# Transposes through two-bank PSUM tiles, norm gains stored by row, and moved norms and weights in a two-layer decoder trunk

## The chip, the cores and the metric

The kernel runs on one core of one Trainium2 chip. The metric is the device time of one execution in microseconds (us). Three runs of the kernel before took 2549.63 us in the median (2548.11 to 2550.36). About 0.2% is what a measurement of it can tell from no change.

## The reference

Two layers over 1024 tokens of width 1024, all in float32:

```python
for layer in range(2):
    hn = rms_norm(h, norm_mix[layer])
    h = h + (diff_attention if layer == 0 else gla)(hn, ...)      # 8 heads / 4 heads
    h = h + conv_ffn(rms_norm(h, norm_ffn[layer]), w_up, conv_w, conv_b, w_down)
return rms_norm(h, norm_final)

def rms_norm(x, gain):   # in float32
    return x * lax.rsqrt(jnp.mean(x * x, axis=-1, keepdims=True) + 1e-6) * gain

def diff_attention(...):     # per head: q, k, v = h @ w_qkv; rope on q and k; two causal softmaxes
    a = p[0] - lam * p[1]
    o = rms_norm(a @ v, subln_gain) * (1 - lambda_init)           # then all heads @ w_o

def conv_ffn(h, ...):        # d_ff = 2816
    u = causal_depthwise_conv(h @ w_up, width=3) + conv_b
    gate, up = jnp.split(u, 2, axis=-1)
    return (silu(gate) * up) @ w_down
```

## The kernel before, in words

**Numbers.** Every factor of a large product is split into a high and a low part, and a product is three matmuls into one float32 PSUM tile (`mm3`, L142 to L144: high by high, low by high, high by low). ACT writes the high part by a copy, DVE or POOL the low part by a subtraction. This is so for weights (`split_w`, L122 and L123; `UpWeights.block`, L477 and L478), for the normed activations (`XH` and `XL`) and for what the heads give (`gh` and `gl`).

**PSUM.** There are two pools, eight banks in all: `psm`, four tiles of one bank of 128x512 (`mm_ps`), and `psb`, two tiles of two banks of 128x1024 (`big_ps`). A tile is given out again when all readers of its last use are done.

**Order.** A scheduler orders the instructions of each engine when the kernel is built. `in_order` (L135) binds pieces of TensorE's work behind one another by hand. Weights of the projections are loaded two ahead (`prefetch`, L106). All loads and stores go through SP's queue.

**The start.** Eight blocks `xt` of x (128 tokens each) are loaded, with the gain of the first norm between the first and the second (`load_gain`, L165, which reads one row of 4 KB into all 128 partitions). Per block ACT squares (L170), DVE and POOL make `rs` (L172, L174), DVE scales to `hn` (L179), TensorE transposes (L202), ACT and DVE write XH and XL. Then come the q and k products of the first head, `stack_q` and `stack_k` (which set the two maps of a head one below the other by DMA; the low parts `ql` and `kl` are POOL's), and v.

**Attention, last head.** `finish` (L796) squares one half of a head's output; its closure `rest` (norm by rows, `rstd_rows`, and the write through `proj.put`) is kept in `later`. Beside the last head's blocks runs the output projection's first part over k = 0 and 1 (`first_units`). After the heads, `OutProjection.rest` (L395) adds k = 2, 3, 4 for tiles 2 and 6 (`accumulate_tiles`, four banks), runs what is left of the last head's norm, and goes on with tiles 3, 7, 0, 4, 1, 5 one by one.

**The block transposes.** In the second half of `rest`, k = 5, 6, 7 are added for tiles t and t + 4 in turn. ACT squares the tile into a two-bank tile (`squares`), and the normed rows `h0` and `h1` are cut into halves. The FFN's up-projection uses a seven-product scheme on blocks, so the operands are not only A11, A12 (`first_row`) and A22 but also the sums S1 to S4 (`Blocks.sums`). Each is transposed by `Blocks.put` (L230): four 128x128 transposes into one bank, one ACT copy, one or two DVE subtractions. That is 28 transposes for each t of 0 to 3. The last five operands of t = 3 (`last_blocks`) come between the first products of the FFN's unit f = 0.

**The FFN.** For each of 22 units f: products `ps_x`, `ps_y`, `ps_z`, and meanwhile the seven weight blocks of f + 1 (`UpWeights.sums`, `others`; DVE L486 to L493). Then the down-projection adds groups of units, (0, 1) first, tile by tile, `accumulate_tile` into two of the four single banks.

Of the kernel before, what the change touches and what calls it, by code (L numbers as in the profile page):

```python
# [46 lines left out]
def trunk(ctx, tc, x, norm_mix, norm_ffn, norm_final, wqk, wv, w_o, lam_in, subln,  # L47
# [117 lines left out]
    def load_gain(src):  # L165
        return staged(src.broadcast_to([P, D]))
# [45 lines left out]
    class Blocks:  # L212
# [17 lines left out]
        def put(self, n, src, t):  # L230
            pt = mm_ps("pt")
# [4 lines left out]
            for (k, hi), (_, lo) in zip(*self.parts(n)):  # L236
                ks = pv[:, k:k + hi.shape[1], :]
                nc.scalar.copy(hi[:, :, tok], ks)
                nc.vector.tensor_tensor(lo[:, :, tok], ks, f32(hi[:, :, tok]), op=ALU.subtract)  # L239
# [17 lines left out]
        def others(self, blocks, t):  # L257
            for n, src in blocks:
                self.put(n, src, t)
# [29 lines left out]
    def accumulate_tiles(res, ts, pairs):  # L289

        ps = [mm_ps("pacc") for _ in range(2 * len(ts))]
# [41 lines left out]
    class OutProjection:  # L333
# [35 lines left out]
        def first_units(self):  # L369
# [14 lines left out]
            def unit(t):  # L384
# [5 lines left out]
                if t == late[0]:  # L390
                    self.prepare((2,))
            return [begin] + [lambda t=t: unit(t) for t in (*early, *late)]

        def rest(self, gain_src, up):

            layer, res = self.layer, self.res
            self.prepare((3, 4))
            pairs = [self.pairs[k] for k in (2, 3, 4)]
            for n, t in enumerate((2, 6, 3, 7, 0, 4, 1, 5)):
                if n != 1:  # L400
                    with in_order(n == 0):
                        (accumulate_tiles(res, (2, 6), pairs) if n == 0 else accumulate_tile(res, t, pairs))
                if n == 1:
                    while self.late:
                        with in_order():
                            self.late.pop(0)()
                if t % 4 > 1:
                    nc.sync.dma_start(r_scr[layer, t], res[t])
# [93 lines left out]
    def ffn(layer, X, last_blocks, up, gain_src, after):  # L502
# [65 lines left out]
        for f in range(NF):  # L568
# [5 lines left out]
            if f + 1 < NF:  # L574
                up.sums(f + 1)
# [56 lines left out]
    def rope_stack_units(h, st, parts=False):  # L632
# [31 lines left out]
        def stack_k():  # L664
            kl = slot(12, "kl", F32R)
            nc.scalar.copy(KS[0], roped[1])
            nc.gpsimd.tensor_tensor(kl, roped[1], f32(KS[0]), op=ALU.subtract)
# [47 lines left out]
    def attention(st, proj, value_T):  # L715
# [49 lines left out]
        def transposes(h, i, a):  # L765
# [3 lines left out]
            for j0 in range(0, i + 1, 4):  # L769
                n = min(4, i + 1 - j0)  # L770
                pt = mm_ps("pta")
# [24 lines left out]
        def finish(h, hf):  # L796
            o = oT[h]
            a = slot(13, "sq", F32, [P, 2, 512])
            nc.scalar.activation(a[:, 0, :], o, AF.Square)
            on = slot(27, "on")[:, :512]  # L800
            nc.scalar.mul(on, o, st["sub"])
            hl = split_rows(a[:, 0, :], 26)
# [9 lines left out]
            later.append(rest)  # L812
# [10 lines left out]
        for h in range(HEADS):  # L823
# [17 lines left out]
            if h + 1 == HEADS:  # L841
                drain()
                proj.late = later
# [470 lines left out]
```

## Time and profile before

| what | us |
|---|---|
| median of three runs | 2549.63 |
| the profiled execution | 2550.43 |
| its span, first to last instruction | 2548.7 |
| TensorE busy (PE) | 2459.1 (96%) |
| VectorE busy (DVE) | 1617.3 (63%) |
| GpSimd busy (POOL) | 1183.6 (46%) |
| ScalarE busy (ACT) | 1041.2 (41%) |
| mean granted TensorE clock | 0.985 |

The span and the median are read against one another thus: the profiled execution lies 0.80 us above the median, and 1.73 us of it lie outside the span. A row of the view by stretches gives, for each engine, its busy time and its instructions in brackets, then the mean granted TensorE clock, the busy share of the DMA engines and what they moved. A row of the timeline gives the start, the time, the engine, the line, the operation, the tile written and those read, the sizes, the count, and in brackets the engine's idle time ahead of it and what ended that.

### The profile page before, as it was taken

The page shows a single profiled execution, that of the slowest core. Times are in us where ns is not written, and L with a number is a line of the kernel's source. Part 1 is how long each engine was busy: PE and PEld are TensorE (multiplying, and loading weights), DVE is VectorE, ACT ScalarE, POOL GpSimd, SP SyncE. Part 2 cuts the span into 40 slices and gives each one's busy share as a digit, 9 for nine tenths or more (in the row PEclk, how much of TensorE's full clock was granted, in tenths as well). Part 3 has the DMA queues.
Part 4 walks back from the last instruction along what each step waited for, and adds up shares of the span by engine and source line. Part 5 has one row for each costly group of instructions (what it writes and reads, how often), then busy time and mean ns, then how long its engine had stood idle before and what let it go on. Part 6 is the DMA issues. An engine that isn't in the chain of part 4 may idle for free. (4 is left out here: it accounts for less than half of the span.)

```text
span 2548.7 us, 30815 instructions
## 1 busy us (share of the span) xinstructions
PE 2459.1 (96%) x11752; PEld 2001.0 (79%) x11752; DVE 1617.3 (63%) x2218; ACT 1041.2 (41%) x1638; POOL 1183.6 (46%) x723
## 2 busy tenths in 40 slices
PE   7999999988899999999999999998889999999998
PEld 5777777767688888878888998987768888887887
DVE  5577777875666666655565576487566666665445
ACT  4454445543454445421124443442345544443211
POOL 3444444424555555545423344343455555555441
PEclk9999999999899999999999999999989999999999
DMA  5222222433122222343321111124212222234331
GB/s 178 63 67 59 59 58 59 126 126 108 66 86 80 83 77 90 126 156 116 100 86 59 34 42 58 34 91 157 100 66 87 79 83 77 89 129 154 114 100 66
DMA packets 66020, 228.61 MB, mean 90 GB/s; under 512 B 8144, under 2 KB 8784, under 8 KB 65872
## 3 DMA queue, kind: packets, MB, share of 16 engines
q1 hardware_dynamic: 65872, 226.64, 27.0%
q8 instruction: 92, 1.51, 0.3%
q14 instruction: 56, 0.46, 0.1%
HBM read 163.17 MB, written 50.86 MB: 84 GB/s over the span
## 5 line engine op out<-in xcount | busy, mean ns | idle before, releaser
L308 DVE TENSOR_TENSOR res<-pacc,res 128x512 f32<-128x512 f32 x408 | 279.4, 689 | 271.5 <-PE pacc L144 271.0
L478 POOL TENSOR_TENSOR uw<-st,uw 128x512 fp32r<-128x512 f32 x190 | 288.4, 1518 | 240.6 <-ACT uw L477 227.7
L123 POOL TENSOR_TENSOR wl<-st,wh 128x1024 fp32r<-128x1024 f32 x55 | 140.2, 2554 | 211.7 <-ACT wh L122 207.8
L142 PE MATMUL pacc<-wdh,gh 128*128 128x512 f32 x512 | 200.2, 393 | 4.0 <-DVE res L308 4.0
L143 PE MATMUL pacc<-wdl,gh 128*128 128x512 f32 x512 | 201.7, 394 | 0.1
L144 PE MATMUL pacc<-wdh,gl 128*128 128x512 f32 x512 | 201.6, 394 | 0.0
L557 DVE SCALAR_TENSOR_TENSOR b<-cu,cv,b 128x1023 f32<-128x1023 f32 x44 | 62.4, 1419 | 186.7 <-ACT b L556 186.7
L477 ACT CAST uw<-st 128x512 fp32r<-128x512 f32 x190 | 118.1, 622 | 112.8 <-PE ps_z L144 55.6
L142 PE MATMUL psq<-XH,wh 128*128 128x512 f32 x384 | 156.1, 407 | 1.2 <-DVE ms L172 1.2
L604 POOL TENSOR_TENSOR gl<-st,gh 128x1024 fp32r<-128x1024 f32 x32 | 78.8, 2463 | 164.5 <-ACT gh L603 121.9
L143 PE MATMUL psq<-XL,wh 128*128 128x512 f32 x384 | 153.9, 401 | 0.8 <-DVE ms L172 0.7
L144 PE MATMUL psq<-XH,wl 128*128 128x512 f32 x384 | 152.6, 399 | 0.0
L753 ACT ACTIVATE p<-p,nmax 128x256 f32<-128x256 f32 (+7 forms) x128 | 99.0, 776 | 86.7 <-DVE nmax L750 85.5
L142 PE MATMUL pacc<-wh,gh 128*128 128x512 f32 x256 | 106.0, 417 | 18.5 <-DVE XL L239 10.9
L603 ACT CAST gh<-st 128x1024 fp32r<-128x1024 f32 x32 | 33.6, 1050 | 214.8 <-PE pacc L143 141.9
L478 POOL TENSOR_TENSOR wh<-st,wh 128x512 fp32r<-128x512 f32 x56 | 86.1, 1537 | 69.6 <-ACT wh L477 69.6
L142 PEld LDWEIGHTS pacc<-wdh,gh 128*128 128x128 f32 x512 | 96.5, 188 | 26.1 <-DVE res L308 5.3
L478 POOL TENSOR_TENSOR wl<-st,wl 128x512 fp32r<-128x512 f32 x56 | 84.1, 1502 | 66.8 <-ACT wl L477 64.7
L143 PEld LDWEIGHTS pacc<-wdl,gh 128*128 128x128 f32 x512 | 96.6, 189 | 22.9 <-POOL wdl L604 1.0
L144 PEld LDWEIGHTS pacc<-wdh,gl 128*128 128x128 f32 x512 | 96.4, 188 | 21.0
L122 ACT CAST wh<-st 128x1024 fp32r<-128x1024 f32 x59 | 61.6, 1047 | 121.7 <-PE psq L143 51.4
L750 DVE CUSTOM_DVE_ANT_0 p<-s_ps,mask 128x256 f32<-128x256 f32 (+7 forms) x128 | 91.4, 750 | 26.9 <-PE pta L773 22.6
(357 smaller groups left out, 7384.8 us busy)
## 6 DMA issues: line engine op xcount, KB each, us to landing
st<-in_wup_dram SPq DMA_DIRECT2D x88, 512.0 KB, 3.5
g_scr<-a SPq DMA_DIRECT2D x44, 512.0 KB, 2.6
st<-in_wdn_dram SPq DMA_DIRECT2D x44, 512.0 KB, 3.6
st<-g_scr SPq DMA_DIRECT2D x44, 512.0 KB, 3.3
r_scr<-res SPq DMA_DIRECT2D x24, 512.0 KB, 3.2
res<-r_scr SPq DMA_DIRECT2D x24, 512.0 KB, 5.6
st<-in_wqk_dram SPq DMA_DIRECT2D x16, 512.0 KB, 3.6
st<-o_scr SPq DMA_DIRECT2D x13, 512.0 KB, 3.3
```

What stands on the lines that cost most here:

```text
L122: nc.scalar.copy(hi, st)
L123: (eng_lo or nc.gpsimd).tensor_tensor(lo, st, f32(hi), op=ALU.subtract)
L142: nc.tensor.matmul(ps, lhsT=ah, rhs=bh, start=first, stop=False, **kw)
L143: nc.tensor.matmul(ps, lhsT=ah, rhs=bl, start=False, stop=False, **kw)
L144: nc.tensor.matmul(ps, lhsT=al, rhs=bh, start=False, stop=last, **kw)
L308: nc.vector.tensor_tensor(res[t][:, half(dh)], ps, res[t][:, half(dh)], op=ALU.add)
L477: nc.scalar.copy(w[:, half(0)], src)
L478: nc.gpsimd.tensor_tensor(w[:, half(1)], src, f32(w[:, half(0)]), op=ALU.subtract)
L557: nc.vector.scalar_tensor_tensor(u[:, 1:], c[:, :T - 1], cv[:, n, 1:2], u[:, 1:], op0=ALU.mult, op1=ALU.add)
L604: nc.gpsimd.tensor_tensor(lo, st, f32(hi), op=ALU.subtract)
L750: nc.vector.tensor_tensor_reduce(out=pm[:, :w], in0=s_ps[:, :w], in1=st["mask"][:, T - w:], scale=-0.125, scalar=3.0e38, op0=ALU.add, op1= ...
L753: nc.scalar.activation(pm[:, :w], pm[:, :w], AF.Exp, bias=nmax, scale=-1.0, accum_out=sums[:, m:m + 1])
```

## The change

1. The gains of the norms lie in memory as 128 equal rows, and `load_gain` reads 512 KB instead of one row of 4 KB.
2. `prefetch()` at the start leaves the low parts of the first two weights to POOL instead of DVE.
3. `stack_q` and `stack_k` of the first head use DVE instead of POOL for `ql` and `kl`.
4. The closures of the last head's `finish` go to `proj.late`, with places in memory of their own for the second half; the last block's transposes use a two-bank tile.
5. `accumulate_tiles` uses all eight banks, for four tiles (2, 6, 3, 7) instead of two, and so do the first groups of the down-projection. In layer 1, k = 3 is prepared in `first_units`.
6. `first_row` transposes eight times into one two-bank tile, with one copy and one subtraction of 128x1024. S3 and S1 (for t = 3 all operands) use the halves of a two-bank tile.
7. The weight sums of f = 1 are bound behind the last blocks' copy and subtraction.

```diff
     def load_gain(src):
-        return staged(src.broadcast_to([P, D]))
+        return staged(src)
...
         def first_row(self, h0, t):
-            for i, n in enumerate(("A11", "A12")):
-                self.put(n, h0[:, half(i)], t)
+            pt = big_ps("pt")
+            for k in range(KT):
+                nc.tensor.transpose(pt[:, k * P:(k + 1) * P], h0[:, k * P:(k + 1) * P], ident)
+            pv = pt.rearrange("p (a b) -> p a b", a=KT)
+            hi, lo = (z[:, :, t * P:(t + 1) * P] for z in (XH, XL))
+            nc.scalar.copy(hi, pv)
+            nc.vector.tensor_tensor(lo, pv, f32(hi), op=ALU.subtract)
...
         def others(self, blocks, t):
-            for n, src in blocks:
-                self.put(n, src, t)
+            big = None
+            for i, (n, src) in enumerate(blocks):
+                if t == 3 or n in ("S3", "S1"):
+                    if big is None:
+                        big = big_ps("pt2")
+                        pt, big = big[:, half(0)], big[:, half(1)]
+                    else:
+                        pt, big = big, None
+                else:
+                    pt = mm_ps("pt")
+                self.put(n, src, t, pt)
...
     def accumulate_tiles(res, ts, pairs):
-        ps = [mm_ps("pacc") for _ in range(2 * len(ts))]
+        ps = [mm_ps("pacc") for _ in range(4)]
+        for _ in range(2):
+            big = big_ps("pacc2")
+            ps += [big[:, half(0)], big[:, half(1)]]
...
+                if t == late[1] and self.base:
+                    self.prepare((3,))
...
-            self.prepare((3, 4))
+            self.prepare((4,) if self.base else (3, 4))
...
-            for n, t in enumerate((2, 6, 3, 7, 0, 4, 1, 5)):
...
+            with in_order(True):
+                accumulate_tiles(res, (2, 6, 3, 7), pairs)
+            for t in (2, 6, 3, 7):
+                nc.sync.dma_start(r_scr[layer, t], res[t])
+            while self.late:
+                with in_order():
+                    self.late.pop(0)()
+            for t in (0, 4, 1, 5):
+                with in_order():
+                    accumulate_tile(res, t, pairs)
...
             if f + 1 < NF:
-                up.sums(f + 1)
+                with ExitStack() as behind:
+                    for i in () if f else X.last:
+                        behind.enter_context(tc.issue_after(i.ins))
+                    up.sums(f + 1)
...
+            if fs[0] == 0:
+                for t in (0, 4):
+                    accumulate_tiles(res, range(t, t + 4), [pairs[f] for f in fs])
+                continue
...
-            nc.gpsimd.tensor_tensor(QL, roped[0], f32(QH[0]), op=ALU.subtract)
+            (nc.vector if parts else nc.gpsimd).tensor_tensor(QL, roped[0], f32(QH[0]), op=ALU.subtract)
...
-            later.append(rest)
+            (proj.late if h == HEADS - 1 else later).append(rest)
...
-            prefetch(nc.vector)
+            prefetch()
```

The rest of the diff: `kl` as `ql`, `finish` with slots 17, 18, 19 for the last half, `pt` handed to `put`, which keeps its last copy and subtraction in `X.last`, and `_rows`, which writes a gain out 128 times on the host's side of the layout.

What moves, at three places. First POOL, at the end of the first head's q, k and v products (`sh`, `qr`, `kr` are the rotation's steps, `wl` the low part of the v weights). Before:

```order
L651 TENSOR_TENSOR sh<-sh,sin 128x512
L659 TENSOR_TENSOR ql<-qr,qh_146 128x1024
L652 TENSOR_TENSOR kr<-kr,sh 128x512
L667 TENSOR_TENSOR kl<-kr,ks_148 128x1024
L123 TENSOR_TENSOR wl<-st,wh 128x1024
```

and now DVE there, where POOL goes from `kr` straight to `wl`:

```order
L676 TENSOR_TENSOR kr<-psq,cos 128x512
L123 TENSOR_TENSOR wl<-st,wh 128x1024
L685 TENSOR_TENSOR ql<-qr,qh_146 128x1024
L693 TENSOR_TENSOR kl<-kr,ks_148 128x1024
L776 ISA p_533,nmax<-s_ps,mask 128x128
```

`ql` no longer stands between two steps of the rotation, and `kl` has left POOL's queue.

Second PE, in the block transposes of the first t (`hn` are the normed rows and their sums in place, `tmp` is S3, `pacc` the accumulation of the next tile; after the first row of transposes, stretches of `pacc` matmuls are left out). Before:

```order
L233 MATMUL pt<-ident,hn 128x128 x8
...
L144 MATMUL pacc<-wh,gl 128x512
L233 MATMUL pt<-ident,hn 128x128 x8
L233 MATMUL pt<-ident,tmp 128x128 x4
L233 MATMUL pt<-ident,hn 128x128 x8
L142 MATMUL pacc<-wh,gh 128x512
```

and now, with 18, 9 and 9 matmuls of `pacc` in the three gaps:

```order
L244 MATMUL pt<-ident,hn 128x128 x8
...
L232 MATMUL pt<-ident,hn 128x128 x12
...
L232 MATMUL pt_5411<-ident,tmp 128x128 x4
...
L232 MATMUL pt_5411<-ident,hn 128x128 x4
L244 MATMUL pt<-ident,hn 128x128 x8
```

The 20 transposes in one run have become 12, 4 and 4 with matmuls between them, and the last 4 stand right ahead of the next tile's first eight.

Third DVE, between the first two products of unit f = 0 and the last blocks (L252 and L253, now L256 and L257, are sums of blocks; L486 to L493, now L505 to L512, the weight sums of f = 1; `cg` drains `ps_y`). Before:

```order
L253 TENSOR_TENSOR hn<-hn 128x512
L486 TENSOR_TENSOR st<-st 128x512
L487 TENSOR_TENSOR st<-st 128x512
L488 TENSOR_TENSOR st<-st 128x512
L493 TENSOR_TENSOR st<-st 128x512
L527 TENSOR_TENSOR cg<-ps_y,rv 128x512
L239 TENSOR_TENSOR XL<-pt,XH 128x4x128
```

and now:

```order
L257 TENSOR_TENSOR hn<-hn 128x512
L546 TENSOR_TENSOR cg<-ps_y,rv 128x512
L238 TENSOR_TENSOR XL<-pt_5763,XH 128x4x128
L238 TENSOR_TENSOR XL<-pt_5663,XH 128x4x128
...
L505 TENSOR_TENSOR st<-st 128x512
L506 TENSOR_TENSOR st<-st 128x512
L507 TENSOR_TENSOR st<-st 128x512
```

The four weight sums have gone behind the last blocks' subtractions.

## Rows read from the trace of the kernel before

**Rows 1.** The page, part 1: busy time of TensorE.

```profile
PE 2459.1 (96%) x11752; PEld 2001.0 (79%) x11752; DVE 1617.3 (63%) x2218; ACT 1041.2 (41%) x1638; POOL 1183.6 (46%) x723
```

**Rows 2.** Busy time by stretches, core 0; after the engines clock, DMA share, GB/s.

```profile
0.00:21.20 21.20, 7.47 (x32) 5.85 (x32) 11.25 (x20) 13.42 (x23) 3.46 (x8) 1.00 0.89 343
54.50:100.00 45.50, 41.98 (x175) 31.17 (x173) 18.56 (x49) 15.49 (x34) 24.14 (x17) 0.89 0.32 82
526.00:560.00 34.00, 27.27 (x133) 21.88 (x133) 27.05 (x35) 15.46 (x22) 12.07 (x6) 0.90 0.37 124
597.00:668.00 71.00, 54.51 (x253) 43.93 (x252) 50.56 (x75) 30.91 (x68) 42.31 (x35) 0.86 0.32 108
1092.00:1106.00 14.00, 11.05 (x42) 8.68 (x41) 14.00 (x11) 5.58 (x6) 8.62 (x4) 0.88 0.45 141
1755.00:1775.00 20.00, 13.83 (x50) 10.25 (x49) 15.17 (x17) 6.20 (x8) 6.67 (x3) 0.83 0.57 190
1811.00:1880.00 69.00, 53.74 (x244) 42.83 (x244) 49.72 (x75) 30.86 (x67) 42.08 (x35) 0.85 0.30 100
2290.00:2335.00 45.00, 43.87 (x189) 34.90 (x188) 28.28 (x32) 18.28 (x19) 34.45 (x13) 1.00 0.69 240
...
2340.00:2500.00 160.00, 160.00 (x694) 130.03 (x693) 77.42 (x112) 28.07 (x28) 66.63 (x28) 1.00 0.27 86
```

**Rows 3.** The page, part 5: DVE's drains of `pacc` (busy, mean ns; idle before).

```profile
L308 DVE TENSOR_TENSOR res<-pacc,res 128x512 f32<-128x512 f32 x408 | 279.4, 689 | 271.5 <-PE pacc L144 271.0
```

**Rows 4.** Timeline of the start, all engines.

```profile
1.63 0.42 SPq L101 DMA_DIRECT2D st<-in_norm_mix_dram  x1
...
8.52 1.28 DVE L179 SCALAR_TENSOR_TENSOR hn<-xt,rs,st 128x1024 f32<-128x1024 f32 x1 [2.69 <-DMA st<-in_norm_mix_dram]
...
17.54 1.22 DVE L123 TENSOR_TENSOR wl<-st,wh 128x1024 fp32r<-128x1024 f32 x1
...
21.24 0.47 PE L142 MATMUL psq<-XH,wh 128*128 128x512 f32 x1 [1.17 <-DVE ms L172]
```

**Rows 5.** Timeline of the first head: POOL, then DVE, then PE.

```profile
50.25 2.16 POOL L652 TENSOR_TENSOR qr<-qr,sh 128x512 f32<-128x512 f32 x1
...
54.53 3.39 POOL L659 TENSOR_TENSOR ql<-qr,qh 128x1024 fp32r<-128x1024 f32 x1
57.89 1.28 POOL L652 TENSOR_TENSOR kr<-kr,sh 128x512 f32<-128x512 f32 x1
60.33 2.40 POOL L667 TENSOR_TENSOR kl<-kr,ks 128x1024 fp32r<-128x1024 f32 x1 [1.16 <-ACT ks L666]
...
49.28 1.97 DVE L123 TENSOR_TENSOR wl<-st,wh 128x1024 fp32r<-128x1024 f32 x1
...
63.92 0.66 PE L681 MATMUL psw<-ident,vt 128*128 128x128 f32 x4 [0.95 <-ACT vt L675]
67.15 0.68 PE L740 MATMUL s_ps<-ks,qh 128*128 128x128 f32 x2 [2.57 <-DMA ks<-kl]
```

**Rows 6.** Timeline at the end of the last head: DVE, then PE.

```profile
533.44 2.29 DVE L286 SCALAR_TENSOR_TENSOR sq<-sq 128x512 f32<-128x512 f32 x1
...
542.86 1.97 PE L773 MATMUL pta<-ident,p 128*128 128x128 f32 x8 [3.94 <-DVE res L308]
```

**Rows 7.** Timeline of the block transposes, layer 0: PE, then DVE.

```profile
609.18 0.47 PE L142 MATMUL pacc<-wh,gh 128*128 128x512 f32 x1 [2.76 <-DVE XL L239]
...
642.78 1.09 PE L233 MATMUL pt<-ident,hn 128*128 128x128 f32 x8 [2.88 <-DVE XL L239]
...
659.02 1.09 PE L233 MATMUL pt<-ident,tmp 128*128 128x128 f32 x4 [4.55 <-DVE cg L527]
...
650.97 1.78 DVE L486 TENSOR_TENSOR st<-st 128x512 f32<-128x512 f32 x1
```

**Rows 8.** Timeline of PE: first down group of layer 0, projection of layer 1.

```profile
1100.56 0.50 PE L142 MATMUL pacc<-wdh,gh 128*128 128x512 f32 x1 [2.95 <-DVE res L308]
...
1765.96 0.80 PE L142 MATMUL pacc<-wh,gh 128*128 128x512 f32 x1 [5.17 <-ACT gh L128]
```

More of the change, by code (lines that the diff above doesn't have):

```diff
@@ L228, in operand, with put @@
             return v[:, k - first, :]
-        def put(self, n, src, t):
-            pt = mm_ps("pt")
+        def put(self, n, src, t, pt):
             for k in range(4):
@@ L237, in put @@
                 ks = pv[:, k:k + hi.shape[1], :]
-                nc.scalar.copy(hi[:, :, tok], ks)
-                nc.vector.tensor_tensor(lo[:, :, tok], ks, f32(hi[:, :, tok]), op=ALU.subtract)
+                self.last = (nc.scalar.copy(hi[:, :, tok], ks),
+                             nc.vector.tensor_tensor(lo[:, :, tok], ks, f32(hi[:, :, tok]), op=ALU.subtract))
         def first_row(self, h0, t):
-            for i, n in enumerate(("A11", "A12")):
-                self.put(n, h0[:, half(i)], t)
+            pt = big_ps("pt")
[5 more added lines that the diff above has]
+            nc.vector.tensor_tensor(lo, pv, f32(hi), op=ALU.subtract)
         def sums(self, h0, h1, t):
@@ L396, in rest @@
             layer, res = self.layer, self.res
-            self.prepare((3, 4))
+            self.prepare((4,) if self.base else (3, 4))
             pairs = [self.pairs[k] for k in (2, 3, 4)]
-            for n, t in enumerate((2, 6, 3, 7, 0, 4, 1, 5)):
[L400 to L408, printed above, removed]
+            with in_order(True):
[8 more added lines that the diff above has]
+                    accumulate_tile(res, t, pairs)
             self.prepare((5, 6, 7))
@@ L666, in stack_k @@
             nc.scalar.copy(KS[0], roped[1])
-            nc.gpsimd.tensor_tensor(kl, roped[1], f32(KS[0]), op=ALU.subtract)
+            (nc.vector if parts else nc.gpsimd).tensor_tensor(kl, roped[1], f32(KS[0]), op=ALU.subtract)
             dma(KS[1][up], KS[0][up])
@@ L770, in transposes @@
                 n = min(4, i + 1 - j0)
-                pt = mm_ps("pta")
+                if h == HEADS - 1 and i == NT - 1:
+                    pt = big_ps("pta")[:, half(0)]
+                else:
+                    pt = mm_ps("pta")
                 for j in range(j0, j0 + n):
@@ L797, in finish @@
             o = oT[h]
-            a = slot(13, "sq", F32, [P, 2, 512])
+            ia, ion, ihl = (17, 18, 19) if h == HEADS - 1 and hf else (13, 27, 26)
+            a = slot(ia, "sq", F32, [P, 2, 512])
             nc.scalar.activation(a[:, 0, :], o, AF.Square)
-            on = slot(27, "on")[:, :512]
+            on = slot(ion, "on")[:, :512]
             nc.scalar.mul(on, o, st["sub"])
-            hl = split_rows(a[:, 0, :], 26)
+            hl = split_rows(a[:, 0, :], ihl)
             def rest():
@@ L842, in attention @@
                 drain()
-                proj.late = later
             value_T = next_v
@@ L1183, in trunk @@
             nc.sync.dma_start(ident, ident_in)
-            gain = load_gain(norm_mix[0:1, :])
+            gain = load_gain(norm_mix[0])
         if t == 3:
-            prefetch(nc.vector)
+            prefetch()
     attention_consts(st)
@@ L1206, in trunk @@
     up = UpWeights(0)
-    X, last_blocks = proj.rest(norm_ffn[0:1, :], up)
+    X, last_blocks = proj.rest(norm_ffn[0], up)
     def keep(t, hn, res):
@@ L1215, in trunk @@
     up = UpWeights(1)
-    X, last_blocks = proj2.rest(norm_ffn[1:2, :], up)
+    X, last_blocks = proj2.rest(norm_ffn[1], up)
     def store(t, hn, res):
@@ L1254, in _units, with _rows @@
     return s
+def _rows(w):
+    return np.ascontiguousarray(np.broadcast_to(w[:, None, :], (w.shape[0], P, D)))
 def _moving(w):
```

8 lines of the change are left out of this document (4 added, 4 removed).

## The prediction, made before the changed kernel was run

> **What bounds the kernel now.** I read the page's busy shares first: TensorE is busy for 2459.1 of 2548.7 us [rows 1], so the program is TensorE's work plus 89.6 us in which it stands still, plus what it loses at half clock. Then the view by stretches. From 2340 to 2500 us 694 matmuls fill 160.00 us without a gap, 0.231 us each [rows 2]; no edit of other engines can gain anything there, and most of the program is like that. What can be gained lies in few stretches, and for each the reader takes two numbers from its row: length less PE busy, which is idle, and (1 - clock) times length, which is work lost to the lower of the two clock levels (1.2 instead of 2.4 GHz: a stretch at half clock shows 0.50). From the rows [rows 2]:
>
> - 0 to 21.2 us: 13.7 idle. 54.5 to 100: 3.5 idle, 5.0 clock.
> - 526 to 560: 6.7 idle, 3.4 clock.
> - 597 to 668 (block transposes, layer 0): 16.5 idle, 9.9 clock.
> - 1092 to 1106: 3.0 idle, 1.7 clock.
> - 1755 to 1775: 6.2 idle, 3.4 clock.
> - 1811 to 1880 (block transposes, layer 1): 15.3 idle, 10.3 clock.
> - 2290 to 2335: 1.1 idle, no clock.
>
> That is 66 us idle and 34 us of clock, 100 us in all: the most that a change of these places could give. The half clock comes behind stalls (of 2.57, 2.76, 3.94 and 5.17 us, [rows 5 to 8]). The third view is the timeline around each stall, which says what ended it: most often DVE, whose drain of one PSUM bank takes 0.69 us [rows 3] and which has other work in its queue.
>
> **The change, part by part.** Gains are negative, and ends of each are given for the range.
>
> *Start (edits 1 and 2).* The first `hn` waits 2.69 us for the gain and starts at 8.52 [rows 4], though the load was issued at 1.63: 6.9 us. TensorE's first transposes need it. As plain rows the gain is one more 512 KB load behind x's first block, so I expect it to be there when `rs` is. It is also ahead of the next three blocks of x. DVE then loses two `wl`, one of them the 1.22 us at 17.54, which stand ahead of the first psq at 21.24 [rows 4]; POOL gets two of some 2.4 us (the length of `kl`, which has that size, [rows 5]) in a queue that otherwise holds `rs`. Sum: 2.69 from the first link and up to 2.4 from DVE, but ACT's squares and copies go one behind the other in the same stretch (13.42 us busy of 21.2, [rows 2]) and become the next limit. I take -2.5. Ends: 0 (POOL's `wl` hold up what DVE gives back) and -5.1 (both in full).
>
> *First head (edit 3).* Before, POOL does `ql` (3.39 us from 54.53), only then the last `kr` (57.89), then `kl` (2.40 from 60.33), and TensorE waits 0.95 us for `vt` and 2.57 us for the DMA of `kl`, which lands at 67.15, 4.4 us behind `kl`'s end [rows 5]. Half clock follows (5.0 us). With `ql` off POOL, `kr` moves up by 3.4 us; `kl` on DVE takes about 1.2 us (`wl` on DVE, same size, [rows 4]) instead of 2.40. So `kl` is done some 4.5 us earlier, and the wait of 2.57 goes with its clock loss: up to -7.6. The 0.95 stays. I take -6.5; ends -3 (the wait goes, the clock stays low for a while) and -8.5 (all).
>
> *Here a rule speaks against it.* The row shows `wl` on DVE at 1.97 us while POOL's `qr` takes 2.16 us instead of `kr`'s 1.28 [rows 5]: the two slow each other. The Trainium skill, page "SBUF — State Buffer", section "Who interferes with whom", says that DVE and GpSimd share a port pair by an exclusive lock: a DVE operation with two SBUF inputs waits for a whole GpSimd instruction. The trace agrees. By that rule `ql` on DVE would wait for `kr`, and `hn` for each `wl` now on POOL; that is the rival of the lock below.
>
> *Last head (edit 4, and the eight banks of `rest`).* DVE does five norm steps among the last block's work, one of them 2.29 us long [rows 6]; TensorE waits 3.94 us for a bank that a drain on DVE frees [rows 6]. At 0.69 us for a plain step of 512 columns on DVE (taken from the drain, [rows 3]), the five are 0.69 x 4 + 2.29 = 5.0 us, more than the wait. They move behind the eight-bank group, where the 72 matmuls of tiles 0, 4, 1, 5 (16.6 us at 0.231) lie beside eight drains (5.5 us) and some 12 steps (8.3 us): 13.8 us fit into 16.6. So the 3.94 and its 3.4 us of clock go, 7.3 in all; the eight-bank group may itself wait for drained banks and for POOL's `wl`, which I put at 2 us back. I take -5.5; ends -1 and -9.
>
> *Block transposes, layer 0 (edits 6 and 7).* This is the largest term. Before, 20 transposes go in one run through four single banks, and each bank must be copied by ACT and subtracted by DVE before it comes back: TensorE waits so once in each of the first three t (2.76 us at 609.18 to 2.88 at 642.78, [rows 7]), and 4.55 us at 659.02 for `cg`, which stands in DVE's queue behind the four weight sums that begin at 650.97 [rows 7]. Now the run is 12, 4 and 4 with 9 matmuls (2.1 us) between. There are new waits too: S1's four transposes share a tile with S3 and wait for its subtraction; `first_row` needs a two-bank tile, so it stands behind `squares`, and one copy and one subtraction of 1024 columns (1.22 us for DVE's, as `wl`) instead of two of 512. I walked the new order with the durations of the rows: stalls of 1.8 and 1.4 us in the first t, 0.45 and 1.2 in the second, none in the third, 0.65 and 3.4 before the first ps_x, 0.8 and 0.95 at the last blocks: 10.7 us in place of 16.5. Only the 3.4 is as long as those that half clock followed; to be careful I leave half of the clock's loss, 5.0 of 9.9 us. Sum: -5.8 - 4.9 = -10.7. Ends: -4.5 (only the wait for `cg` goes) and -16 (the walk, with hardly any drop).
>
> *Block transposes, layer 1.* The same code in the same order; its wait for `cg` is shorter, so I take -10; same ends.
>
> *First down group.* In layer 0 TensorE waits 2.95 us at 1100.56 for a drain [rows 8], with 1.7 us of clock behind it; eight banks give 5.5 us of cover (24 matmuls) instead of 2.8. I take -3, ends 0 and -4.7. In layer 1 1.1 us of idle: -0.8.
>
> *Projection of layer 1 (edit 5).* TensorE waits 5.17 us for ACT's `gh` of k = 3 at 1765.96 [rows 8], with 3.4 us of clock. Now k = 3 is prepared a unit earlier, and 48 matmuls of k = 2 and 3 (11.1 us) stand ahead of k = 4 instead of 24. I take -5.5; ends 0 (another preparation is late in its place) and -9.
>
> *At nothing.* The gains' larger reads (the later ones are loaded long before use), and the moved stores of residual rows on SP. Without that cover a late gain would cost as the first one did, 2.7 us.
>
> **Sum.** -2.5 - 6.5 - 5.5 - 10.7 - 10 - 3 - 0.8 - 5.5 = -44.5 against the profiled execution of 2550.43: 2505.9. That execution lies 0.80 above the median, so I say **2506 us** for the median. All least ends together give -13 (2537), all largest -69 (2481); such a coincidence is unlikely, so the likeliest case alone spans 2490 to 2522.
>
> **Rivals.**
>
> *The ring is still too small.* Only two two-bank tiles exist, and `squares`, `first_row`, S3 with S1 and the first `ps_z` all want them; with stalls staying near 2.7 us the clock falls as before, and each layer gives only its -4.5. For it: every stall before was a wait for a PSUM tile. Against: there are now matmuls between the pieces. Time: 2506 + 6.2 + 5.5 = 2518.
>
> *The lock.* POOL's `wl` at the start hold DVE's `hn`, and `ql` waits on POOL's rotation: the start gives 0 and the first head -3. Time: 2506 + 2.5 + 3.5 = 2512. For it: the 1.97 and 2.16 us [rows 5]; against: POOL is nearly empty before 21 us (3.46 us busy, [rows 2]).
>
> *The clock stays up.* No stall is as long as those that half clock followed before, and the 5 us that I left in each layer come back too: 2506 - 10 = 2496; with full gains elsewhere 2490.
>
> *Slower.* The chain through `first_row` becomes serial: drain 0.69, squares and copy of 1024 columns (each put at the 1.22 of DVE's step of that size), eight transposes, subtraction 1.22, on one of two tiles, for each of the eight t. If each t then stalls twice for 2.8 us and runs as after 67 us (5.0 us lost), it costs 10.6 us, 85 in all, in place of 52 now: +33 against -24 from the other parts, 2559. It decides from about 9.5 us per t on, against 6.5 now. The interleaving speaks against it.
>
> *It does not do what it says.* The scheduler might have kept the old order. The order of PE, DVE and POOL shows the moves, so this has hardly a chance.
>
> **How the numbers follow.** Forecast 0.63, ring 0.16, lock 0.10, clock 0.07, slower 0.02, no effect 0.02. The range takes in the likeliest case, the ring and the lock with a few us on either side, and most of the clock's case: **2489 to 2529**. About 0.2% (5 us) is what a measurement can tell from no change. Faster by more: 0.95; within: 0.03; slower by more: 0.02.
>
> **What would show it.** Right: the first psq near 18.5 us; no wait for `kl`'s DMA and no half clock behind it; no wait of 3 us for a drain at the end of the last head; the two stretches of block transposes shorter by about 10 us each, with half the loss of clock; no wait for `cg` above 1 us; full clock through both first down groups. Wrong: waits for `XL`, `squares` or S blocks of 2.5 us and more in every t; a new wait of DVE's `hn` beside POOL's `wl`; the norms moved behind the eight-bank group holding up its successors.

## The result, and the profile after

The changed kernel takes 2519.11 us in the median of four runs (2511.29 to 2519.34), the kernel before 2549.79 beside it: a ratio of 0.9876, with a 95% interval of 0.9858 to 0.9894. It is 31 us faster, inside the range of 2489 to 2529, and 13 us short of the 2506 that the sum gave. The profiled execution took 2519.34 us, its span is 2517.6. The quickest of the four, 8 us ahead of the others, has a mean granted clock of 0.995, the others 0.991 to 0.993, and 0.004 of the span are 10 us. No trace of the quickest was kept, so where its clock stayed up is not shown. The parts below are judged by stages of the profile first, and by the whole time only where the interval allows. One execution of the run on the norms of the last head (3989.89 us, mean granted clock 0.557) was in a slow state and is left out of its median.

The page's first part, and of TensorE's waits in the changed kernel (total, times, longest) those that the text below speaks of:

```profile
PE 2450.1 (97%) x11752; PEld 1995.8 (79%) x11752; DVE 1625.7 (65%) x2210; ACT 1040.6 (41%) x1630; POOL 1189.4 (47%) x723
```

```profile
PE pt L232 <- DVE S L238: 6.0, 6, 1.3
PE pacc L142 <- DVE res L325: 4.0, 2, 3.8
PE ps_x L142 <- ACT rv L556: 3.7, 2, 2.1
...
PE pta L802 <- DVE p L785: 3.0, 2, 2.5
...
PE s_ps L766 <- DMA ks<-kl: 2.4, 1, 2.4
```

TensorE stands still for 67.5 us instead of 89.6 [rows 1]. The waits for XL of 2.7 to 2.9 us [rows 7], for the drain at the end of the last head [rows 6], for `cg` and for `gh` [rows 8] are gone. In their place are longer waits for S blocks (6.0 us in all, none over 1.3), short ones of 1.7 us and less for other pieces of the transposes, a drain in layer 1 (3.8), and waits for ACT's `rv` and for `p`, under whose names the list of the kernel before has none. The wait for the DMA of `kl` [rows 5] has stayed.

To compare stage by stage I cut both executions at the same instructions of TensorE: first psq, first scores, first pacc of the last head, first block transpose, first ps_z, first down-projection, and the same in layer 1. Columns are those of [rows 2], where the first stretch before stands. Before:

```profile
21.20:67.10 45.90, 41.35 (x184) 32.46 (x184) 22.31 (x40) 14.21 (x23) 23.21 (x15) 0.96 0.37 102
67.10:100.00 32.90, 32.85 (x132) 24.13 (x132) 16.71 (x47) 11.25 (x28) 14.73 (x12) 0.85 0.17 46
495.40:598.10 102.70, 94.14 (x427) 72.80 (x426) 72.16 (x114) 37.88 (x63) 22.81 (x13) 0.97 0.32 106
598.10:666.00 67.90, 51.41 (x239) 41.42 (x238) 50.04 (x75) 29.80 (x66) 41.15 (x33) 0.85 0.32 109
666.00:706.00 40.00, 40.00 (x174) 32.49 (x173) 22.31 (x22) 20.47 (x30) 20.30 (x14) 1.00 0.18 55
1077.80:1110.00 32.20, 29.18 (x120) 23.17 (x119) 25.03 (x23) 14.85 (x16) 19.11 (x7) 0.95 0.67 245
1721.80:1809.30 87.50, 79.50 (x349) 63.35 (x349) 53.72 (x70) 19.09 (x24) 22.05 (x12) 0.96 0.39 134
1809.30:1876.30 67.00, 51.74 (x240) 41.37 (x239) 50.41 (x75) 30.24 (x66) 41.59 (x33) 0.85 0.33 109
```

and after:

```profile
0.00:20.10 20.10, 7.59 (x32) 6.27 (x32) 11.56 (x18) 12.19 (x21) 8.74 (x10) 1.00 0.90 346
20.10:63.70 43.60, 40.86 (x183) 32.14 (x181) 25.37 (x40) 14.93 (x24) 17.39 (x14) 1.00 0.38 112
63.70:96.60 32.90, 32.44 (x130) 23.73 (x131) 15.98 (x45) 10.70 (x27) 14.00 (x13) 0.84 0.15 43
492.50:589.50 97.00, 92.26 (x427) 72.34 (x427) 69.33 (x114) 37.51 (x63) 22.42 (x13) 0.98 0.34 112
589.50:647.10 57.60, 48.11 (x239) 38.28 (x238) 43.20 (x68) 28.59 (x60) 37.53 (x30) 0.91 0.33 110
647.10:691.20 44.10, 42.02 (x177) 33.68 (x175) 30.10 (x26) 21.69 (x33) 28.16 (x18) 0.96 0.23 76
1063.00:1091.00 28.00, 27.56 (x121) 22.33 (x119) 21.11 (x17) 11.55 (x13) 13.97 (x5) 1.00 0.60 223
1702.40:1785.30 82.90, 78.74 (x349) 63.89 (x348) 54.18 (x70) 19.10 (x24) 22.63 (x12) 0.96 0.41 140
1785.30:1843.70 58.40, 48.23 (x239) 38.69 (x238) 45.47 (x70) 29.62 (x61) 38.05 (x30) 0.91 0.32 108
```

| part | predicted | measured |
|---|---|---|
| start, up to the first psq | -2.5 | -1.1 |
| first head, up to the first scores and behind them | -6.5 | -2.3 |
| last head and k = 2 to 4 | -5.5 | -5.7 |
| block transposes, layer 0 (to ps_z -10.3, behind it +4.0) | -10.7 | -6.3 |
| first down group, layer 0 | -3 | -4.2 |
| projection of layer 1 | -5.5 | -4.6 |
| block transposes, layer 1 (to ps_z -8.6, behind it +2.3) | -10 | -6.3 |
| first down group, layer 1 | -0.8 | -0.8 |

The measured ones add to -31.3. "Behind it" is where the reader must look past the stage that was changed: for the same work from the first ps_z on (174 to 177 matmuls) layer 0 took 40.0 us without a gap before, and takes 44.1 now, of which 2.1 are idle and (1 - 0.96) of the 44.1, 1.8, are clock.

How much these stages differ from one execution to the next shows in eight of the runs below, which leave the block transposes and the FFN as they are. From the first block transpose to the first ps_x they take 38.5 us in layer 0, all of them. From there to the first ps_z they take 16.7 to 19.5 us (19.1 in the changed kernel), and the 173 matmuls behind it 42.5 to 45.2 (44.1). The whole of this is 100.0 to 102.6 us in layer 0 and 98.9 to 102.8 in layer 1, where the changed kernel has 101.7 and 100.8.

### The profile page after: what moved, and what is told of

The parts are those of the page before. It is cut to its first block, busy times and chain, and to the rows that moved or that the text cites. A ratio compares the mean times of both kernels' runs of the same rounds, so it can differ in the third digit from the quotient of the medians.

```text
span 2517.6 us, 30784 instructions
## 1 busy us (share of the span) xinstructions
PE 2450.1 (97%) x11752; PEld 1995.8 (79%) x11752; DVE 1625.7 (65%) x2210; ACT 1040.6 (41%) x1630; POOL 1189.4 (47%) x723
## 5 line engine op out<-in xcount | busy, mean ns | idle before, releaser
L325 DVE TENSOR_TENSOR res<-pacc,res 128x512 f32<-128x512 f32 x368 | 252.9, 690 | 238.1 <-PE pacc L144 237.6
L123 POOL TENSOR_TENSOR wl<-st,wh 128x1024 fp32r<-128x1024 f32 x57 | 146.0, 2568 | 203.6 <-ACT wh L122 203.6
L143 PE MATMUL pacc<-wl,gh 128*128 128x512 f32 x256 | 102.8, 403 | 1.5 <-POOL wl L123 1.5
```

Source lines behind the costliest of these rows:

```text
L123: (eng_lo or nc.gpsimd).tensor_tensor(lo, st, f32(hi), op=ALU.subtract)
L143: nc.tensor.matmul(ps, lhsT=ah, rhs=bl, start=False, stop=False, **kw)
L325: nc.vector.tensor_tensor(res[t][:, half(dh)], ps, res[t][:, half(dh)], op=ALU.add)
```

## The experiments

Ratios are against the kernel before on the same chip; the changed kernel's is 0.9876 [0.9858, 0.9894].

**The chain of the first scores.** One DMA of the first head is made by ACT.

```diff
-            dma(KS[1][up], KS[0][up])
+            if parts:
+                nc.scalar.copy(KS[1][up], f32(KS[0][up]))
+            else:
+                dma(KS[1][up], KS[0][up])
```

> The changed kernel with one of the first head's DMAs, the copy of KS[0]'s upper half into KS[1]'s, made by ACT (same partitions); all else stays. Theory W (chain of DMAs): the first scores wait for the DMA of kl into KS[0], which may only start when the DMA that reads KS[0] has landed (issues from 56.88 to 61.17 us); without that DMA the last one is issued by 59 us, lands before 61.5, the wait of 2.37 us goes, and with it the 10 us at half clock (5.1 us): 2511.5 to 2517 us. Theory K (kl's own DMA is what takes 4 to 6 us): the wait stays over 1.5 us, the half clock stays, and the time stays within 1.5 us of the changed kernel's.

2511.72 us, ratio 0.9857 [0.9842, 0.9872], which still overlaps the changed kernel's interval. The changed kernel's timeline of SP's queue and TensorE, and then that of this run, with its stretch behind the first scores:

```profile
56.88 0.59 SPq L681 DMA_DIRECT2D ks<-ks  x1
57.52 3.65 SPq L681 DMA_DIRECT2D ks<-kl  x2
...
63.67 0.53 PE L766 MATMUL s_ps<-ks,qh 128*128 128x128 f32 x2 [2.37 <-DMA ks<-kl]
```

```profile
57.92 1.10 SPq L681 DMA_DIRECT2D ks<-kl  x2
...
62.29 0.42 PE L769 MATMUL s_ps<-ks,qh 128*128 128x128 f32 x2 [0.57 <-DMA ks<-kl]
```

```profile
62.30:95.00 32.70, 32.15 (x148) 24.27 (x149) 17.75 (x51) 13.40 (x33) 19.69 (x15) 1.00 0.22 57
```

The two issues of `kl` took 3.65 us, since the second, which overwrites KS[0], waits for the landing of the DMA that reads it. Without that DMA they take 1.10, the wait is 0.57, and the clock stays up (1.00 instead of 0.84), so nearly the same time holds 148 matmuls instead of 130. Theory W, as expected: of the traces of this study the clock falls behind the first scores in all ten without ACT's copy, and in none of the four with it. The size of that loss differs from one execution to the next, though. The last run of this section has the same order as the changed kernel and the same wait of 2.37 us, and in its stretch

```profile
64.20:97.10 32.90, 32.44 (x142) 24.14 (x143) 17.74 (x50) 12.72 (x31) 16.87 (x14) 0.95 0.18 49
```

142 matmuls fit, so 6 to 18 matmuls (1.4 to 4.2 us at 0.231) are the clock's part. The scores themselves start 1.4 us earlier, or 2.1 counted from the first psq.

The reverse, `ql` and `kl` on POOL again (edit 3 undone):

```diff
-            (nc.vector if parts else nc.gpsimd).tensor_tensor(QL, ...)
+            nc.gpsimd.tensor_tensor(QL, ...)
```

> The changed kernel with ql and kl of the first head on POOL again; all else stays. Theory W (chain of DMAs, from the run with the copy on ACT): what bounds the first scores is the pair of DMAs that read and write KS[0], so DVE's faster kl bought only what kr's earlier end moved that chain: the first scores come 0.5 to 2.5 us later and the half clock behind them stays as it is: 2519 to 2522 us. Theory P (the edit is worth what the prediction gave it): 5 to 7 us are given back: 2524 to 2526 us.

2518.07 us, 0.9877 [0.9861, 0.9894]. The first scores start at 65.52 instead of 63.67, with a wait of 2.58, and half clock follows as before. The edit is worth 1.9 us at its place (1.5 counted from the first psq), and the whole time, which came out 1 us below what W gives, does not show it: theory W again, not P.

**The lock between DVE and POOL.** The low parts of the prefetched weights of both output projections go to DVE.

```diff
-                    w = load_w(self.w_out[k])
+                    w = load_w(self.w_out[k], nc.vector)
```

> The changed kernel with the low parts of the prefetched output-projection weights (both layers) on DVE instead of POOL; all else stays. Theory L (DVE and POOL hold each other up): p L785 takes about 1.2 us instead of 3.14 beside POOL's two wl of 5.66 us together, the wait of 2.50 us for it at the end of the last head falls under 1 us, layer 1's wait of 3.8 us for a drain (DVE L300 2.78 and L1132 3.32 beside POOL's wl of 5.40) falls under 1.5 us, and their half clock (1.7 and 2.5 us) goes: 2510 to 2515 us. Theory D (DVE is simply full there): DVE's own two wl of 1.2 us each take the place, the waits stay within 1 us of 2.5 and 3.8: 2517 to 2521 us.

2507.44 us, 0.9835 [0.9820, 0.9849]. At the end of the last head, in the changed kernel (DVE, POOL), and then in this run (DVE), with its two stretches up to the first block transpose of each layer:

```profile
532.64 3.14 DVE L785 SCALAR_TENSOR_TENSOR p<-p,rc,p 128x1024 f32<-128x1024 f32 x1
...
532.33 5.66 POOL L123 TENSOR_TENSOR wl<-st,wh 128x1024 fp32r<-128x1024 f32 x2 [1.08 <-ACT wh L122]
```

```profile
530.20 1.27 DVE L785 SCALAR_TENSOR_TENSOR p<-p,rc,p 128x1024 f32<-128x1024 f32 x1
531.40 2.35 DVE L123 TENSOR_TENSOR wl<-st,wh 128x1024 fp32r<-128x1024 f32 x2
```

```profile
490.10:583.00 92.90, 90.79 (x427) 71.02 (x427) 71.81 (x118) 37.64 (x63) 12.05 (x9) 1.00 0.36 117
1696.50:1772.70 76.20, 76.14 (x349) 62.29 (x349) 52.68 (x75) 19.11 (x24) 13.65 (x8) 1.00 0.46 153
```

The same step takes 1.27 us instead of 3.14, and the two subtractions 2.35 on DVE instead of 5.66 on POOL. In layer 0 DVE is busy for 71.81 us instead of 69.33 and the stage ends earlier; in layer 1 even its busy time falls, from 54.18 to 52.68. The stages shrink by 4.1 and 6.7 us (97.0 to 92.9, 82.9 to 76.2), layer 1's to TensorE's bare work. Theory L, by more than expected. In layer 1 of the changed kernel, where TensorE waits 3.8 us for a drain that stands behind them, the lengthened steps are

```profile
1739.28 2.78 DVE L300 SCALAR_TENSOR_TENSOR sq<-sq 128x512 f32<-128x512 f32 x1
1742.10 3.32 DVE L1132 TENSOR_TENSOR r<-r,sq 128x512 f32<-128x512 f32 x2
```

which take 0.69 and 1.29 us with the subtractions on DVE. How the two engines hold each other up can be read from POOL's two subtractions at 532 us one by one (shortest, median and longest in ns, then first and last start):

```profile
L123 POOL TENSOR_TENSOR wl<-st,wh x2: 2362/2858/3355, 532.3 to 534.6; 128x1024 fp32r<-128x1024 f32 x2
```

The first takes 2.36 us, no more than such a step of POOL alone (2.40, [rows 5]), and ends at 534.7. `p`, which began beside it, ends 1.1 us later, at 535.8. The second subtraction, begun at 534.6, ends 2.2 us behind `p`. By these times each step got little or nothing done until the other's was over. The Trainium skill, page "SBUF — State Buffer", section "Who interferes with whom", calls this an exclusive lock: a DVE instruction with two inputs in SBUF contends with a GpSimd instruction that reads SBUF. The trace agrees. The lock was a rival in the prediction for the start and the first head, and it bound most at two places where I had not looked for it.

It was there before the change too, which I had overlooked. In the kernel before, the drain that ended TensorE's wait of 3.94 us [rows 6] stood right behind the same `p`, beside the same two subtractions of POOL:

```profile
538.84 3.36 DVE L759 SCALAR_TENSOR_TENSOR p<-p,rc,p 128x1024 f32<-128x1024 f32 x1
542.13 0.68 DVE L308 TENSOR_TENSOR res<-pacc,res 128x512 f32<-128x512 f32 x1
...
538.67 5.75 POOL L123 TENSOR_TENSOR wl<-st,wh 128x1024 fp32r<-128x1024 f32 x2 [3.49 <-ACT wh L122]
```

The drain itself, which reads PSUM, keeps its 0.68 us beside POOL.

Both of these edits together:

> The changed kernel with both the ACT copy in the first head (which alone took 2511.7 us) and the low parts of the prefetched output-projection weights on DVE. Where theory L holds for the low parts, the two gains add, since they lie 450 us apart: 2503 to 2508 us. Where theory D holds, 2509.5 to 2513.5 us.

2502.67 us, 0.9816 [0.9802, 0.9831]: they add (0.0019 and 0.0041 of the ratio by themselves, 0.0060 together).

**Where the first two low parts are made.** Edit 2 undone, `prefetch(nc.vector)`:

> The changed kernel with the low parts of the first two weights on DVE again; all else stays. Theory L (DVE and POOL hold each other up): hn of the fourth block on DVE takes 1.3 us again instead of 3.30, rs of the fifth no longer waits for 5.67 us of POOL's wl, and the first psq starts at 19 to 20.5 us instead of 20.14, so the time is the same within 2 us or up to 2 us less. Theory M (POOL is the better place, DVE was the limit): the first psq starts 1.5 to 2.5 us later and the time is 1.5 to 2.5 us longer.

2518.03 us, 0.9883 [0.9868, 0.9897]; the first psq starts at 20.03 instead of 20.14. The changed kernel's DVE and POOL at the start:

```profile
7.01 1.28 DVE L179 SCALAR_TENSOR_TENSOR hn<-xt,rs,st 128x1024 f32<-128x1024 f32 x1 [1.17 <-DMA st<-in_norm_mix_dram]
...
14.94 3.30 DVE L179 SCALAR_TENSOR_TENSOR hn<-xt,rs,st 128x1024 f32<-128x1024 f32 x1
...
14.80 5.67 POOL L123 TENSOR_TENSOR wl<-st,wh 128x1024 fp32r<-128x1024 f32 x2
```

On POOL the two subtractions cost DVE 2.0 us in one `hn` (3.30 instead of 1.28); on DVE they cost 2.4 us themselves, and that `hn` takes 1.28 again. It comes to the same: theory L, and no gain in edit 2.

**The gain by row.** Edit 1 undone in the load alone:

```diff
-        return staged(src)
+        return staged(src[0:1, :].broadcast_to([P, D]))
```

> The changed kernel reading one row of 4 KB into all partitions for each gain again (the gains stay stored 128 times); all else stays. Theory G (the row form was late by itself and held the queue behind it): the first hn starts at 8.5 us again instead of 7.01, the second block's squares at 9.9 instead of 8.52, and the first psq 1 to 2 us later than 20.14: 0.5 to 2 us longer, nothing elsewhere. Theory H (ACT's and DVE's chain over the four blocks sets the start): the first hn is late but psq starts within 0.5 us of 20.14.

2518.67 us, 0.9886 [0.9872, 0.9901]. The first `hn` starts at 8.84 instead of 7.01, the second block's squares at 9.99 instead of 8.52, the first psq at 21.62 instead of 20.14: theory G, 1.5 us at its place, too little for the whole time to show. The size is rough: in the eleven traces with the gain as rows and POOL's two subtractions the first psq starts at 19.45 to 20.87.

**The tiles of two banks.** Edit 6 undone (`first_row` through `mm_ps` in two pieces, `others` through `mm_ps` alone):

```diff
-                if t == 3 or n in ("S3", "S1"):
+                if False:
```

> The changed kernel with the block transposes through the four single banks again (first_row as two tiles, S3 and S1 and all of t = 3 as before); all else stays. Theory R (the two-bank tiles give the gain of the block stage): the waits for XL of 2.7 to 2.9 us come back in every t, with half clock behind them, and the stages from the first block transpose to the first ps_z are 6 to 10 us longer in each layer: 2531 to 2540 us. Theory T (the gain of that stage came from moving the weight sums and from a calmer clock): less than 3 us longer in each layer: 2519 to 2525 us.

2526.94 us, 0.9918 [0.9903, 0.9934], clear of the changed kernel's. Stretches to the first ps_z and behind it in layer 0, then one of the waits:

```profile
591.50:653.40 61.90, 49.53 (x239) 39.55 (x238) 44.47 (x73) 28.56 (x64) 34.06 (x29) 0.89 0.30 102
653.40:700.00 46.60, 43.40 (x176) 34.43 (x175) 31.11 (x25) 21.95 (x33) 29.33 (x19) 0.93 0.21 72
```

```profile
602.68 0.54 PE L142 MATMUL pacc<-wh,gh 128*128 128x512 f32 x1 [2.76 <-DVE XL L238]
```

The waits of 2.7 to 2.9 us are back in each of the first three t, this one to the hundredth [rows 7]. The stage is 4.3 us longer in layer 0 and 3.0 in layer 1, and the 173 matmuls behind ps_z take 2.3 and 1.6 more: 11 us in the profile, 8 in the medians. That is between the theories: the tiles are worth some 6.5 and 4.5 us a layer, not 6 to 10. The whole of it, 108.2 and 105.3 us, lies outside the spread of the eight runs above. Up to the first ps_x layer 0 takes 47.2 us instead of 38.5, but from there to ps_z 14.7 instead of 19.1, so half of the loss comes back. Of these 4.4 us 1.9 are idle time (1.1 instead of 3.0), and the rest is TensorE's busy time, at a mean clock of 0.82 instead of 0.73. That the last blocks no longer share their tiles fits the shorter waits (0.39 and 0.63 us instead of 1.09 and 1.34), but no run tests it by itself.

**The weight sums.** Edit 7 undone:

```diff
-                    for i in () if f else X.last:
+                    for i in ():
```

> The changed kernel (2519.1 us) with the weight sums of f = 1 no longer bound behind the last blocks; all else stays. Theory Q (a queue's work was moved, not removed): the late sums are what makes ACT's copy rv of f = 1 late, so TensorE's waits for rv L556 behind the first ps_z (2.1 us in layer 0, 1.6 us in layer 1, and 1.7 us of half clock) go, and in exchange cg or the last blocks' XL and S waits grow by about as much: 2516 to 2522 us. Theory P (the edit carries what the prediction gave it, 4.55 us in layer 0 and 3.0 us in layer 1): 2524 to 2530 us, with a wait for cg of 3 us or more in each layer.

2521.72 us, 0.9893 [0.9876, 0.9909]. Its stretches to and behind the first ps_z, layer 0 then layer 1:

```profile
590.00:650.80 60.80, 48.69 (x239) 38.65 (x238) 45.75 (x70) 29.79 (x62) 42.94 (x33) 0.89 0.32 106
650.80:691.00 40.20, 40.20 (x177) 32.62 (x176) 23.04 (x23) 20.89 (x31) 19.98 (x14) 1.00 0.23 77
1785.50:1848.30 62.80, 48.47 (x239) 39.01 (x238) 48.01 (x71) 30.18 (x62) 43.36 (x33) 0.89 0.34 116
1848.30:1890.00 41.70, 41.70 (x182) 33.84 (x181) 23.95 (x23) 20.69 (x30) 21.58 (x15) 1.00 0.19 64
```

Unbound, the last blocks are 3.2 and 4.4 us longer, and behind ps_z there is no gap. The wait that the binding had taken away is back, for an XL block: 5.0 us in two pieces in layer 0, 4.8 in one in layer 1. So the price put on edit 7 was that of the wait, and what it gives back behind ps_z was left out. The whole is 101.0 and 102.9 us, inside the spread of the eight runs in layer 0 and at its edge in layer 1, so the binding's worth is nothing that these traces can tell, and the intervals of the whole time overlap: theory Q, at its upper end. In the changed kernel the late chain reads so (DVE, ACT, PE):

```profile
658.37 1.31 DVE L505 TENSOR_TENSOR st<-st 128x512 f32<-128x512 f32 x1 [3.39 <-DMA st<-in_wup_dram]
...
669.90 1.24 ACT L575 ACTIVATE a<-cg,cv 128x1024 f32<-128x1024 f32 x1 [5.15 <-DVE cg L572]
...
671.67 0.50 PE L142 MATMUL ps_x<-XH,uw 128*128 128x512 f32 x1 [2.08 <-ACT rv L556]
```

With f = 1's sums late, those of f = 2 follow late too (3.39 us of waiting for their load), and they stand in DVE's queue ahead of `cg` of f = 0. ACT's queue waits for `cg` for 5.15 us with `rv` behind it, and TensorE needs the bank that `rv` reads.

Two runs take the sums of f = 1 out of DVE's queue, on top of the 2502.67 us:

```diff
+            eng = nc.gpsimd if f == 1 else nc.vector
-            nc.vector.tensor_tensor(t[:, one], r2[:, two], r1[:, one], op=sub)
+            eng.tensor_tensor(t[:, one], r2[:, two], r1[:, one], op=sub)
```

(and so for the other three), first bound as in the change, then not bound.

> The run with the ACT copy and the low parts on DVE (2502.7 us), and the four weight sums of f = 1 on POOL instead of DVE, bound behind the last blocks as before. Theory Q (these sums in DVE's queue, made longer by POOL beside them, keep cg and the gate's a of f = 0 late, so that ACT's rv of f = 1 is late): the waits for rv L556 (2.9 and 3.4 us) and their half clock go, 2494 to 2499 us. Theory O (POOL is the longer way: its sums take 1.3 us each ahead of its low parts): waits for POOL's uw of 2 us and more come instead, 2500 to 2506 us.

> As the run with the four weight sums of f = 1 on POOL, but not bound behind the last blocks, so that they start when the weights are there. Theory Q: no wait for rv and none for cg of over 1 us, 2493 to 2498 us, since DVE's queue holds neither. Theory O: POOL's sums stand ahead of POOL's own step of the last blocks and the last blocks wait for POOL by 2 us or more, 2500 to 2506 us.

2499.68 us, 0.9810 [0.9794, 0.9827], and 2497.45 us, 0.9802 [0.9787, 0.9816]. In both TensorE no longer waits for `rv`. Not bound, layer 0:

```profile
579.50:638.60 59.10, 47.46 (x240) 38.15 (x239) 42.66 (x67) 30.06 (x62) 45.40 (x37) 0.91 0.31 106
638.60:680.00 41.40, 41.40 (x181) 33.60 (x180) 23.77 (x23) 20.79 (x30) 21.92 (x16) 1.00 0.28 89
```

Behind ps_z nothing is lost; to ps_z it is 1.5 us longer than the changed kernel, with a wait of 3.3 us for an S block in the middle of the last blocks. Q holds for `rv`. That wait is a piece of O by another way: ACT's `uw` waits 1.67 us for one of POOL's sums, with the copy of the S block behind it in ACT's queue. The bound run ends between the ranges of Q and O, the other inside Q's. Their intervals overlap each other and that of the 2502.67 us, so a gain over that run is not shown; both are clear of the changed kernel's, some 20 us below it, and 50 below the kernel before.

**The norms of the last head.** Edit 4 undone (the closures in `later`, what is left of them handed to `proj.late`):

> The changed kernel with the last head's norms beside its last blocks again (later instead of proj.late; the places in memory and the two-bank tile stay); all else stays. Theory N (DVE's five steps were what TensorE waited for): a wait of 3 to 4.5 us for DVE comes back at the end of the last head, with longer half clock, the stage from the first pacc of the last head to the first block transpose is 3.5 to 6 us longer: 2522.5 to 2525 us. Theory B (the gain of that stage is the eight banks', the norms only changed places): less than 2 us longer: 2519 to 2521 us.

2520.54 us, 0.9887 [0.9871, 0.9904]. The stage takes 100.2 instead of 97.0 us, with a wait of 3.3 us for `p` instead of 2.5, and `p` takes 3.36 us beside POOL as in the kernel before. By the stage it is short of N and more than B; the whole time lies in B's range, and its interval overlaps the changed kernel's. So of the 5.7 us some 3.2 are the norms'. The rest is left for the eight banks and the two-bank tile of the last block's transposes, which no run undoes.

**The early preparation.** `prepare((3,))` in layer 1 taken back:

> The changed kernel with k = 3 of layer 1's projection prepared after the loop again, the eight banks stay; all else stays. Theory K (the early preparation is what removed the wait of 5.17 us for ACT's gh): that wait comes back, the stage from the first pacc of layer 1's projection to the first block transpose is 4 to 6 us longer than 82.9: 2523 to 2526 us. Theory E (the eight banks removed it, since twice as many matmuls stand ahead of the next k): less than 1.5 us longer: 2517 to 2521 us.

2518.13 us, 0.9884 [0.9868, 0.9901]; the stage takes 82.2 us (82.9 in the changed kernel), with the same wait of 3.8 us for a drain. The order of every engine's work is the same row for row with and without it. So that line of the change moves nothing, and theory K is out. Theory E holds as what is left: no run takes the eight banks away, here or in the first down groups, where no other edit touches the code.

## Why the prediction was right, and where its steps failed

**Right.** The direction and the range; that only a few stretches could give anything; the start in its sign only (-1.1 for -2.5); the last head, both first down groups and layer 1's projection to within 1.5 us each. The walk through the new order of the block transposes said 10.7 us of stalls; the row up to ps_z shows 9.5 (57.6 - 48.1).

The time is close to that of the rival of the ring (2518), but its sign is missing: no stall in the block transposes is over 1.7 us, and the stages up to ps_z gave 10.3 and 8.6 us, not 4.5. The sum was 13 us too large by four terms above all, the start (1.4), the first head (4.2) and the two block transposes (4.4 and 3.7). That the range held all the same is owed to its width of 40 us.

**First head, -6.5 taken, -2.3 measured.** The failed step is "`kl` is done some 4.5 us earlier, and the wait of 2.57 goes with its clock loss". `kl` was done 5.2 us earlier (57.50 instead of 62.73), but a wait of 2.37 stayed, and the clock loss with it (0.84 for 0.85). I had taken the 4.4 us between `kl`'s end and the scores for the transfer of `kl`. In the kernel before that was so; SP's queue issued both of its DMAs without a wait:

```profile
62.76 1.10 SPq L655 DMA_DIRECT2D ks<-kl  x2
```

The copy of KS[0], issued at 60.28, had landed by then. Now it is issued at 56.88, 0.6 us before `kl` is done, its landing becomes the bound, and the scores come only 3.5 us earlier (63.67 instead of 67.15), 1.1 of them from the start. The run with ACT's copy shows what I had taken for edit 3's: the wait goes and the clock stays up. The same DMAs stood in SP's queue of the trace before; I did not ask what else the last of them waits for.

**Block transposes, -10.7 and -10 taken, -6.3 each measured.** Up to ps_z the term held in layer 0 (-10.3), and nearly in layer 1 (-8.6). What failed is edit 7's price: by the wait for `cg` that it takes away, and not by what is late next. The sums of f = 1 and f = 2, `cg`, `rv` and the bank of ps_x gave 4.0 and 2.3 us back behind ps_z. That chain was in no rival.

Of the clock's part the reason failed, while its number came out: "Only the 3.4 is as long as those that half clock followed". In the changed kernel the clock is at 0.51 from 628.0 to 635.0, behind stalls of which none is over 1.7 us, in this stretch (and then the half clock):

```profile
617.00:628.00 11.00, 8.13 (x51) 6.80 (x51) 9.32 (x15) 7.30 (x15) 7.89 (x7) 1.00 0.23 95
628.00:635.00 7.00, 6.43 (x15) 4.72 (x16) 5.77 (x8) 1.89 (x6) 5.52 (x4) 0.51 0.43 132
```

Breaking a long stall into short ones near one another did not keep the clock up. The half that I left to be careful, 5.0 us, came out with luck: (1 - 0.91) of the 57.6 us is 5.2. And (1 - clock) over all of a stretch also counts half clock in idle time, where no work is lost: it fell by 5.0 us (10.2 to 5.2), while TensorE's busy time for the same 239 matmuls fell by 3.3 (51.41 to 48.11).

**The lock.** As a rival I had put it at 6 us, at the start and in the first head. There it holds (3.30 instead of 1.28 us for one `hn`, and 2.31 for `ql` beside POOL's `kr`, where `kl` alone takes 1.23) but costs little, since at the start either engine pays about the same: the two subtractions gave nothing there, and what the start gained is the gain's load. It costs 10.8 us at the ends of the two mixers (4.1 and 6.7), where the prediction spoke of "five norm steps" and put down 2 us back for banks and "POOL's `wl`". The drain waited for in the last head stood behind the norms and behind a `p` made long by POOL; moving the norms left `p`. The term came out right by two errors that offset each other: the stage could give 9.8 us (102.7 to 92.9), not 7.3, and POOL's subtractions kept 4.1 of them, not 2.

**Projection of layer 1.** The size was near (-4.6 for -5.5). Of its two reasons the early preparation is void, and the eight banks are not tested by themselves.

## What to carry to other kernels

Before pricing an edit by the wait that it removes, follow each operand of the waiting instruction one step further: the second to last arrival (here a DMA that must land, and a `p` step held by POOL) is what the gain stops at. A step that is moved behind others is paid by its consumers: read the next pass of the loop too. Where two engines lengthen each other's steps, moving work onto the busier one can be the quicker way (2.35 us on DVE for 5.66 on POOL, a ratio of 0.9835 instead of 0.9876), and a count of each engine's load alone says the opposite.

## What the runs showed of the hardware that I had not expected

A load of one 4 KB row into 128 partitions was slower than 512 KB of rows, for itself and for the loads behind it: the first `hn` came at 7.01 instead of 8.84 us, the second block of x at 8.52 instead of 9.99. Steps of VectorE and GpSimd that both work in SBUF ended one behind the other rather than running side by side (2.36 us for GpSimd's first, `p` 1.1 us later, GpSimd's second 2.2 us after that), while a drain of PSUM on VectorE beside GpSimd kept its 0.68 us. And TensorE's clock fell to half behind several stalls that were each short (0.41 to 1.67 us, with 8.13 of 11.00 us busy). Behind a single stall of 2.37 us in the first head it stayed at half for 10.2 us in the changed kernel (32.9 us at a mean of 0.84), and in another execution of the same order for less long (0.95 over 32.9 us); it stayed at 1.00 when that stall was 0.57.
